# Input norm on one engine, a recurrence's products on VectorE, and two later tails in a hybrid decoder layer

## The chip, the cores and the metric

One core of a Trainium2 chip runs the kernel. The metric is the device time of one execution in microseconds (us). Engines are named as in the profile: PE (TensorE matmul), PEld (its weight load), DVE (VectorE), ACT (ScalarE), POOL (GpSimd), SP (SyncE, here only DMA issue). L12 is line 12 of the kernel.

## The reference

One decoder layer over 512 tokens of width 2048, in float32.

```
xn   = rmsnorm(x, norm_w);  proj = xn @ w_in          # 2048 -> all branches
# branch 1: HGRN2, 8 heads of 128: gated linear recurrence, then a norm per head
S_t  = diag(f_t) S_{t-1} + (1 - f_t) i_t^T ;  o_t = S_t^T q_t
o_hg = rmsnorm(o, hg_norm_w) * silu(z)
# branch 2: NSA, 4 key groups x 4 heads of 128, three attentions added by gates:
#   compressed blocks (31 keys), selected blocks, causal window
o_ns = g0 * softmax(q kc) vc + g1 * softmax(q ks) vs + g2 * softmax(q kw) vw
# merge
y    = x + (sig(m1) * (o_hg @ w_hg) + sig(m2) * (o_ns @ w_nsa)) @ w_out ; out = rmsnorm(y)
```

## The kernel before

Every float32 operand of a projection is split into a rounded high part and the rest, and a product is three matmuls: high x high, low x high, high x low (`mm3`). A weight block of 128 x 1024 is loaded by SP into one of three `wr` buffers, rounded by ACT (L130) and its rest taken by DVE (L131) into one of two `whl` buffers. A split of activations is the same pair, ACT L135 and DVE L136. So PE depends on a steady alternation of ACT and DVE whatever else these two do.

The stages follow one another: the start (L290 to L404, 0 to 61 us), projections that need no side work (to about 440 us), the recurrence (to about 855 us), compression of keys and values and the first branch product (to about 1077 us), the four key groups of NSA (to about 1660 us), the merge and the output product.

In the start, `normalise(i)` takes the square sum of token tile `i` (half on ACT L329, half on DVE L330), adds (DVE L335), takes the root (ACT L336), the reciprocal (DVE L337), and scales the tile by that and by the norm weight `nw`: quarters 0 and 1 in one DVE operation each (L341), quarters 2 and 3 first by `nw` on POOL (L334) and then by the scalar on DVE (L343). `transposed` turns each quarter on PE (L349) and splits it; `first` multiplies it with the first weight blocks.

From the recurrence on, `weave` runs two generators side by side: the projection of the next head or group (the main one), and the steps of the present one (`hg_core`, `nsa_core`), one step per `yield`, spread evenly over the main one's units. A scheduler then orders each engine's instructions, so the order on an engine differs from that in the code.

`hg_core` works on tiles of 128 channels x 512 tokens. `pre` and `suf` are products of decays up to and after a token within a block; `grow(h)` doubles the block, `suf` on POOL (L566) and `pre` on DVE (L567). `decayed(h)` forms the scaled keys (POOL L576) and queries (DVE L577) of a level in one tile `qk`, whose scores are transposed products on PE (L601) into a bank of PSUM, copied under a mask by DVE (L588, L590, L605) into `ad`. Seven levels follow one another. `kd` (POOL L624) and `qd` (DVE L625) serve the state. Last comes the norm of the head's output: ones-product on PE, root on ACT (L670), reciprocal and two products on DVE (L671 to L673), and a DMA issued by POOL (L674). It stands in the step behind the last products of the head, and falls beside the start of the next head.

`nsa_core(g)` does for each of four heads four steps of scores (query block i = 3, 2, 1, 0; L139 into `sc` banks, of which there are two), each followed by a masked maximum on DVE (L921), exponentials on ACT (L925) and a scale on POOL (L930); then six steps that transpose weights on PE (L949), split them (`pth`, `ptl`) and, one step later, multiply them with the values into the bank `po`. At a group's start the compressed part comes first: scores on PE, softmax on DVE and ACT (L864 to L888, tile `pc`), and the compressed values, loaded by ACT's queue (L855) into a tile `raw`, split into `vczh` and `vczl`. `nsa_proj(g)` loads the group's values into `vraw` (L822) and splits them whole.

PSUM has eight banks: three `pj`, two `sc`, two `pt`, one `po`.

## Time and profile before

| what | value |
|---|---|
| median of 3 runs | 2109.39 us (2108.59 to 2112.3) |
| profiled execution | 2108.82 us, span 2106.7 us, mean granted clock 0.996 |
| busy share | PE 98%, PEld 82%, DVE 57%, ACT 39%, POOL 15% |
| PE idle in 20-us windows, 0 to 40 us | 12.0 us |
| PE idle in 520 to 820 us | 7.4 us |
| PE idle in 1140 to 1580 us | 11.8 us |

The span is one profiled execution; the 2.1 us between it and the execution's own time lie outside the trace. PE's busy time is close to the span, so the time is read from where PE is idle. In the views, a bracket behind an instruction gives the idle time of its engine before it and the instruction whose end ended that. A window's row gives the busy time of each engine in it. All rows are of the one profiled execution.

### The profile page before, as it was taken

Reading aid. Unit: us, or ns where it says so; the run is one execution under the profiler, and the core shown is the slowest. Engines: PE = TensorE matmul, PEld = TensorE weight load, DVE = VectorE, ACT = ScalarE, POOL = GpSimd, SP = SyncE. Lnnn points to the kernel's source line nnn. Section 1 sums busy time; section 2 is a strip of 40 time slices with the busy share of each in tenths; the row PEclk is TensorE's granted clock in tenths of the full one; section 3 lists DMA queues with packets and bytes.
Section 4 is the critical chain, followed back from the end, with each engine's and each line's share of the span. In section 5 each row is a group of like instructions: output and inputs, shape, how many; then the busy total and the mean of one; then the engine's idle time right before and its main releaser. Section 6 shows DMA issues by size and latency. Waiting matters only on the chain.

```text
span 2106.7 us, 26671 instructions
## 1 busy us (share of the span) xinstructions
PE 2062.0 (98%) x10304; PEld 1721.2 (82%) x10304; DVE 1209.0 (57%) x1875; ACT 816.5 (39%) x1267; POOL 322.4 (15%) x411
## 2 busy tenths in 40 slices
PE   7999999999999999999999999999999999999998
PEld 6888888888888778878888887877878888888887
DVE  7687778745456655566545665657654453433333
ACT  4454444532233233344323444445445432222232
POOL 2000000003233432100002222213212100000000
PEclk9999999999999999999999999999999999999999
DMA  6325243332323222566752222222223394445232
GB/s 184 100 105 180 100 152 114 121 101 74 96 83 93 76 76 85 167 188 202 247 164 85 74 73 85 68 84 64 78 75 92 90 304 132 149 140 212 98 130 90
DMA packets 306595, 254.46 MB, mean 121 GB/s; under 512 B 10666, under 2 KB 263411, under 8 KB 305827
## 3 DMA queue, kind: packets, MB, share of 16 engines
q1 hardware_dynamic: 282980, 202.55, 31.8%
q0 software_dynamic: 8096, 26.28, 3.4%
q10 hardware_dynamic: 15392, 23.92, 3.3%
q8 instruction: 81, 1.33, 0.3%
q14 instruction: 46, 0.38, 0.1%
HBM read 222.25 MB, written 30.47 MB: 120 GB/s over the span
## 4 chain that ended last, share of the span: by engine, by line
PE 82%; DVE 7%; issue 4%; ACT 3%; DMA 3%; POOL 1%; SPq 0%; ACTq 0%; DVEq 0%; POOLq 0%
PE pj L139 17%; PE pj L141 17%; PE pj L140 17%; PE sc L214 4%; PE pt L214 4%; PE sc L215 2%; PE pt L215 2%; PE sc L141 2%; PE sc L139 2%; PE sc L140 2%; PE po L140 1%; DVE whl L131 1%; PE po L139 1%; PE po L141 1%; PE pt L949 1%
## 5 line engine op out<-in xcount | busy, mean ns | idle before, releaser
L139 PE MATMUL pj<-xhl,whl 128*128 128x512 f32 x1344 | 538.5, 401 | 0.0
L141 PE MATMUL pj<-xhl,whl 128*128 128x512 f32 x1344 | 527.7, 393 | 0.8 <-DVE whl L131 0.8
L140 PE MATMUL pj<-xhl,whl 128*128 128x512 f32 x1344 | 525.2, 391 | 0.0
L131 DVE TENSOR_TENSOR whl<-wr,whl 128x1024 fp32r<-128x1024 f32 x244 | 303.8, 1245 | 373.2 <-ACT whl L130 372.5
L130 ACT CAST whl<-wr 128x1024 fp32r<-128x1024 f32 x244 | 256.5, 1052 | 563.3 <-PE pj L141 446.8
L141 PEld LDWEIGHTS pj<-xhl,whl 128*128 128x128 f32 x1344 | 252.3, 188 | 56.6 <-DVE whl L131 2.0
L140 PEld LDWEIGHTS pj<-xhl,whl 128*128 128x128 f32 x1344 | 252.9, 188 | 46.4
L139 PEld LDWEIGHTS pj<-xhl,whl 128*128 128x128 f32 x1344 | 252.7, 188 | 46.1
L135 ACT CAST whl<-xt 128x1024 fp32r<-128x1024 f32 x75 | 78.6, 1052 | 97.7 <-PE pt L215 33.1
L136 DVE TENSOR_TENSOR whl<-xt,whl 128x1024 fp32r<-128x1024 f32 x75 | 91.5, 1223 | 39.3 <-ACT whl L135 39.2
L930 POOL TENSOR_SCALAR s<-s,sm 128x512 f32<-128x512 f32 (+3 forms) x128 | 82.2, 655 | 149.4 <-DVE sm L928 89.9
L139 PE MATMUL pj<-onh,whl 128*128 128x512 f32 x256 | 99.6, 389 | 0.0
L140 PE MATMUL pj<-onl,whl 128*128 128x512 f32 x256 | 99.6, 389 | 0.0
L141 PE MATMUL pj<-onh,whl 128*128 128x512 f32 x256 | 99.6, 389 | 0.0
L136 DVE TENSOR_TENSOR ptl<-pt,pth 128x512 fp32r<-128x512 f32 (+1 forms) x80 | 50.5, 633 | 69.3 <-ACT pth L135 68.6
L925 ACT ACTIVATE s<-s,mx 128x512 f32<-128x512 f32 (+3 forms) x128 | 70.9, 555 | 43.8 <-DVE mx L923 39.0
L135 ACT CAST pth<-pt 128x512 fp32r<-128x512 f32 (+1 forms) x80 | 43.5, 544 | 96.1 <-PE pt L949 95.7
L201 DVE TENSOR_TENSOR xt<-xt 128x1024 f32<-128x1024 f32 x64 | 77.5, 1219 | 0.6
L921 DVE CUSTOM_DVE_ANT_0 s<-sc,cf 128x512 f32<-128x512 f32 (+3 forms) x128 | 59.3, 483 | 20.1 <-PE sc L141 19.4
L698 POOL TENSOR_TENSOR rsh<-rsh,rope 32x512 f32<-32x512 f32 x28 | 42.2, 1507 | 183.8 <-DVE rsh L697 166.3
L566 POOL TENSOR_TENSOR suf<-suf,pre 128x256 f32<-128x256 f32 x56 | 51.8, 926 | 116.7 <-DVE pre L549 94.6
L131 DVE TENSOR_TENSOR cl<-wr,ch 128x1024 fp32r<-128x1024 f32 x32 | 39.1, 1223 | 44.6 <-ACT ch L130 44.6
(431 smaller groups left out, 4004.9 us busy)
## 6 DMA issues: line engine op xcount, KB each, us to landing
wr<-in_w_in_dram SPq DMA_DIRECT2D x172, 512.0 KB
xt<-in_w_in_dram SPq DMA_DIRECT2D x32, 1024.0 KB
wr<-in_w_branch_nsa_dram SPq DMA_DIRECT2D x32, 512.0 KB
wr<-in_w_out_dram SPq DMA_DIRECT2D x32, 512.0 KB
wr<-in_cmp_k_w_dram SPq DMA_DIRECT2D x16, 512.0 KB
wr<-in_w_branch_hg_dram SPq DMA_DIRECT2D x16, 512.0 KB
wr<-in_cmp_v_w_dram SPq DMA_DIRECT2D x16, 512.0 KB
gat_d<-wr POOLq DMA_DIRECT2D x20, 256.0 KB, 3.0
```

The source lines that it names most:

```text
L130: nc.scalar.copy(hi[:, :n], raw[:, :n])
L131: nc.vector.tensor_tensor(lo[:, :n], raw[:, :n], hi[:, :n].bitcast(F32), op=OP.subtract)
L135: nc.scalar.copy(hi, src)
L136: nc.vector.tensor_tensor(lo, src, hi.bitcast(F32), op=OP.subtract)
L139: nc.tensor.matmul(acc, lhsT=lh, rhs=rh, start=start, stop=False, **kw)
L140: nc.tensor.matmul(acc, lhsT=lh, rhs=rl, start=False, stop=False, **kw)
L141: nc.tensor.matmul(acc, lhsT=ll, rhs=rh, start=False, stop=stop, **kw)
L201: nc.vector.tensor_tensor(dst, dst, more, op=OP.add)
L214: nc.tensor.matmul(av, lhsT=l0, rhs=r, start=start, stop=False, skip_group_check=True)
L215: nc.tensor.matmul(av[:, 0], lhsT=l1, rhs=r[:, 0], start=False, stop=stop, skip_group_check=True)
L925: nc.scalar.activation(s[:, b], s[:, b], AF.Exp, scale=SCALE, bias=mx[:, b:b + 1], accum_out=sm[:, b:b + 1])
L930: nc.gpsimd.tensor_scalar(s[:, b], s[:, b], sm[:, b:b + 1], 1.0, op0=OP.mult, op1=OP.mult)
```

## The change

Four edits. (1) `normalise` scales all four quarters in one DVE operation each; the POOL product goes. (2) In the recurrence `suf`, the scaled keys and `kd` are formed by DVE. (3) The norm of a head is put into a list and done in the next head's steps behind its copy `kn`; the last head's at once. (4) In NSA the value products of a step are put into a list `due` and done later, those of the last steps in the next head's score steps; the compressed part's transposes stand one step earlier; one of the two score products of block 2 uses a `pj` bank; a group's values are loaded and split in two halves through the `raw` tiles; side steps are 46 and not 48.

```diff
@@ normalise
-            for k0 in (8, 12):
-                c = slice(k0 * P, (k0 + 4) * P)
-                nc.gpsimd.tensor_tensor(x[:, c], x[:, c], nw[:, c], op=OP.mult)
...
-                if k0 < 8:
-                    nc.vector.scalar_tensor_tensor(x[:, c], x[:, c], ss[:, :1], nw[:, c], op0=OP.mult, op1=OP.mult)
-                else:
-                    nc.vector.tensor_scalar(x[:, c], x[:, c], ss[:, :1], None, op0=OP.mult)
+                nc.vector.scalar_tensor_tensor(x[:, c], x[:, c], ss[:, :1], nw[:, c], op0=OP.mult, op1=OP.mult)
@@ hg_core
-                nc.gpsimd.tensor_tensor(fv[:, :, 0], fv[:, :, 0], whole(pv[:, :, 1]), op=OP.mult)
+                nc.vector.tensor_tensor(fv[:, :, 0], fv[:, :, 0], whole(pv[:, :, 1]), op=OP.mult)
...
-                nc.gpsimd.tensor_tensor(half(qk)[:, :, 0], half(kt)[:, :, 0], half(suf)[:, :, 0], op=OP.mult)
+                nc.vector.tensor_tensor(half(qk)[:, :, 0], half(kt)[:, :, 0], half(suf)[:, :, 0], op=OP.mult)
...
-            nc.gpsimd.tensor_tensor(kd, kt[:, :3 * P], suf[:, :3 * P], op=OP.mult)
+            nc.vector.tensor_tensor(kd, kt[:, :3 * P], suf[:, :3 * P], op=OP.mult)
...
             nc.scalar.copy(kn, ps[:, :3 * P])
             yield
+            if left:
+                left.pop()()
             yield
...
-            pm = lbank()
...
-            nc.gpsimd.dma_start(ohg_d[head], ow)
+            def normed():
+                pm = lbank()
...
+                nc.gpsimd.dma_start(ohg_d[head], ow)
+
+            left.append(normed)
+            if head == HG - 1:
+                left.pop()()
@@ nsa_proj
-        raw = ap.tile([P, 4, 2, DH], F32, name="vraw")
-        for b in range(2):
-            nc.scalar.dma_start(raw[:, :, b], v_d[1 + b, :, :, g * DH:(g + 1) * DH].rearrange("i p c -> p i c"))
...
-        split(f(vh), f(vl), f(raw))
+        for b in range(2):
+            raw = ap.tile([P, S], F32, name="raw", bufs=2)
+            rv = raw.rearrange("p (i c) -> p i c", i=4)
+            nc.scalar.dma_start(rv, v_d[1 + b, :, :, g * DH:(g + 1) * DH].rearrange("i p c -> p i c"))
+            split(vh[:, :, b], vl[:, :, b], rv)
@@ nsa_core
+        due = []
+        def pv_next():
+            if not due:
+                return
+            h, po, parts, hi, lo, last = due.pop(0)
+            for n, (j, b) in enumerate(parts):
+                w = slice(n * (4 - j) * P, (n + 1) * (4 - j) * P)
+                mm3(po[:, j * P:], vh[:, j, b], vl[:, j, b], hi[:, w], lo[:, w], False, last)
+            if last:
...
+                if i > 1:
+                    pv_next()
...
-                        ps = sbank()
+                        ps = bank() if i == 2 and b == 0 else sbank()
...
+                if h == 0 and i == 1:
+                    cmp_t()
...
-                    if pend:
-                        pv_mm(*pend, False)
-                    pend = (parts, hi, lo)
+                    if m == 2:
+                        po = psum("po")
+                        mm3(po, vcz[0][:, h], vcz[1][:, h], ph, pl, True, False)
+                    elif m > 2:
+                        pv_next()
+                    due.append([h, None, parts, hi, lo, m == 5])
...
+        while due:
             yield
+            pv_next()
+        yield
```

The program's order on DVE in the start, before and after the change (`xhl` are splits of a transposed quarter, `wfl` rests of the first weight blocks, the first `sq` is token tile 1's):

```order
-L330 SCALAR_TENSOR_TENSOR sq_269,ss<-xt 128x1024
-L343 TENSOR_SCALAR xt<-xt,ss 128x512 x2
-L335 TENSOR_TENSOR ss<-ss 128x1
-L337 RECIPROCAL ss<-ss 128x1
-L341 SCALAR_TENSOR_TENSOR xt<-xt,ss,nw 128x512 x2
-L131 TENSOR_TENSOR wfl<-wraw,wfh 128x1216
-L136 TENSOR_TENSOR xhl<-pt,xhl 128x4x128
```

```order
+L337 SCALAR_TENSOR_TENSOR xt<-xt,ss,nw 128x512 x4
 L131 TENSOR_TENSOR wfl<-wraw,wfh 128x1216
 L136 TENSOR_TENSOR xhl<-pt,xhl 128x4x128
 L131 TENSOR_TENSOR wfl<-wraw,wfh 128x1216
 L136 TENSOR_TENSOR xhl<-sc,xhl 128x4x128
```

Tile 0's last two quarters stood behind tile 1's square sum and now stand with the first two, ahead of the first weight block's rest.

DVE at the start of a head of the recurrence, before (`kt`, `pre` and `qf` begin the new head, `ob` and `ow` belong to the norm of the old one):

```order
L547 TENSOR_SCALAR kt<-sg,nomlb,omlb 128x512
L549 TENSOR_SCALAR pre<-sg,omlb,lbt 128x512
L552 TENSOR_TENSOR qf<-qf,pre 128x4x64
L671 RECIPROCAL ob<-ob 128x512
L567 TENSOR_TENSOR pre<-pre 128x256
L131 TENSOR_TENSOR whl<-wr,whl 128x1024
L672 SCALAR_TENSOR_TENSOR ow<-ow,sv,ob 128x512
L577 TENSOR_TENSOR qk<-qf,pre 128x128x2
L673 TENSOR_TENSOR ow<-ow,zs 128x512
```

The same place in the changed program, and then the place that the norm has come to, behind `kd` and `qd`, where the state `st` is formed:

```order
L542 TENSOR_SCALAR kt<-sg,nomlb,omlb 128x512
L544 TENSOR_SCALAR pre<-sg,omlb,lbt 128x512
L547 TENSOR_TENSOR qf<-qf,pre 128x4x64
L561 TENSOR_TENSOR suf<-suf,pre 128x256
L562 TENSOR_TENSOR pre<-pre 128x256
L571 TENSOR_TENSOR qk<-kt,suf 128x128x2
L572 TENSOR_TENSOR qk<-qf,pre 128x128x2
```

```order
L620 TENSOR_TENSOR qd<-qf,pre 128x384
L131 TENSOR_TENSOR whl<-wr,whl 128x1024 x2
L670 RECIPROCAL ob<-ob 128x512
L131 TENSOR_TENSOR whl<-wr,whl 128x1024
L671 SCALAR_TENSOR_TENSOR ow<-ow,sv,ob 128x512
L645 SCALAR_TENSOR_TENSOR st<-st,pre,sc 128x128
L672 TENSOR_TENSOR ow<-ow,zs 128x512
```

The old head's reciprocal and two products no longer stand among the new head's first operations; `suf` and the keys of `qk` stand there in their place.

ACT at the border from key group 0 to 1, before (`vh` are the group's values, `vczh` the compressed ones, `pc` the compressed scores, `s` the exponentials):

```order
L135 CAST vh<-vraw 128x1024
L130 CAST whl<-wr 128x1024
L178 ACTIVATE raw<-pj 128x512
L822 DMA vraw<-v_d 128x4x128
L855 DMA raw<-vc_d 31x128 x4
L864 COPY pc<-sc 128x512
L822 DMA vraw<-v_d 128x4x128
L135 CAST vczh<-raw 128x512
L879 ACT_TABLE_LOAD
L879 ACTIVATE pc<-pc 128x512
```

The same place in the changed program:

```order
L178 ACTIVATE raw<-pj 128x512
L828 DMA raw<-v_d 128x4x128
L135 CAST vh<-raw 128x4x128
L867 COPY pc<-sc 128x512
L828 DMA raw<-v_d 128x4x128
L858 DMA raw<-vc_d 31x128 x4
L135 CAST vh<-raw 128x4x128
L882 ACT_TABLE_LOAD
L882 ACTIVATE pc<-pc 128x512
L130 CAST whl<-wr 128x1024
L135 CAST vczh<-raw 128x512
L946 ACTIVATE s_9847,sm<-s_9847,mx 128x512 x2
```

A cast of `vh` now stands behind the DMA that brings its half, ahead of the copy of the compressed scores, and `vczh` has moved from ahead of the softmax of `pc` to between it and the first exponentials.

## Rows read from the trace of the kernel before

**Rows 1.** The page, part 1: busy time and share of the span.
```profile
PE 2062.0 (98%) x10304; PEld 1721.2 (82%) x10304; DVE 1209.0 (57%) x1875; ACT 816.5 (39%) x1267; POOL 322.4 (15%) x411
```

**Rows 2.** View of waits of PE: total us, times, longest us.
```profile
PE sc L139 <- DVE mx L921: 8.9, 6, 2.5
PE sc L601 <- DVE ad L605: 7.4, 7, 1.3
PE pt L349 <- DVE xt L341: 3.6, 1, 3.6
PE pt L349 <- DVE xt L343: 1.7, 1, 1.7
PE po L140 <- DVE ptl L136: 1.6, 3, 0.5
```

**Rows 3.** View of windows, the start: length, busy us (instructions) by engine, PEclk, DMA.
```profile
12.00:18.50 6.50, 6.49 (x25) 5.96 (x26) 5.73 (x7) 3.23 (x5) 0.00 (x0) 0.50 0.50 140
18.50:28.80 10.30, 5.98 (x30) 4.74 (x29) 8.47 (x9) 4.82 (x8) 5.31 (x4) 0.83 0.80 271
28.80:45.00 16.20, 13.22 (x94) 12.28 (x93) 15.88 (x22) 10.38 (x17) 6.78 (x5) 1.00 0.42 109
45.00:62.00 17.00, 16.83 (x117) 15.92 (x116) 16.60 (x23) 5.08 (x14) 0.00 (x0) 1.00 0.20 53
```

**Rows 4.** Timeline of POOL in the start: start, length, instruction, [idle before <-releaser].
```profile
18.62 5.31 POOL L334 TENSOR_TENSOR xt<-xt,nw 128x512 f32<-128x512 f32 x4 [7.45 <-issue]
```

**Rows 5.** Timeline of DVE in the start, same columns.
```profile
11.21 1.41 DVE L341 SCALAR_TENSOR_TENSOR xt<-xt,ss,nw 128x512 f32<-128x512 f32 x2 [2.67 <-POOL nw L305]
...
19.93 2.88 DVE L343 TENSOR_SCALAR xt<-xt,ss 128x512 f32<-128x512 f32 x2 [1.88 <-POOL xt L334]
...
22.73 1.22 DVE L335 TENSOR_TENSOR ss<-ss 128x1 f32<-128x1 f32 x1
...
25.84 1.42 DVE L131 TENSOR_TENSOR wfl<-wraw,wfh 128x1216 fp32r<-128x1216 f32 x1
...
32.47 0.68 DVE L136 TENSOR_TENSOR xhl<-pt,xhl 128x512 fp32r<-128x512 f32 x1
...
41.38 0.47 DVE L343 TENSOR_SCALAR xt<-xt,ss 128x512 f32<-128x512 f32 x1
```

**Rows 6.** Timeline of POOL behind the recurrence.
```profile
865.35 1.67 POOL L698 TENSOR_TENSOR rsh<-rsh,rope 32x512 f32<-32x512 f32 x1 [7.94 <-DMA rope<-in_cf_dram]
```

**Rows 7.** View of windows, a head of the recurrence.
```profile
720.00:740.00 20.00, 18.88 (x102) 16.02 (x101) 18.20 (x28) 3.64 (x4) 13.06 (x15) 1.00 0.25 75
```

**Rows 8.** Timeline of DVE, the same head.
```profile
718.87 3.34 DVE L671 RECIPROCAL ob<-ob 128x512 f32<-128x512 f32 x1
...
722.13 0.36 DVE L567 TENSOR_TENSOR pre<-pre 128x256 f32<-128x256 f32 x1
...
730.53 0.72 DVE L605 COPY_PREDICATED ad<-cm,sc 128x256 f32<-128x256 uint8 x1
...
746.55 1.22 DVE L131 TENSOR_TENSOR whl<-wr,whl 128x1024 fp32r<-128x1024 f32 x1 [6.28 <-ACT whl L130]
```

**Rows 9.** View of line L577 (queries of a level): ns min/median/max.
```profile
L577 DVE TENSOR_TENSOR qk<-qf,pre x48: 412/731/955, 479.7 to 823.7; 128x256 f32<-128x256 f32 x48
```

**Rows 10.** View of lines, POOL, 440 to 860 us: count | busy us, mean ns.
```profile
L566 POOL TENSOR_TENSOR suf<-suf,pre 128x256 f32<-128x256 f32 x56 | 51.8, 926 | 116.7 <-DVE pre L549 94.6 <-DVE pre L567 20.1 <-DVE ad L590 0.2
L576 POOL TENSOR_TENSOR qk<-kt,suf 128x256 f32<-128x256 f32 x48 | 44.2, 921 | 17.9 <-PE sc L601 6.3 <-PE pt L601 6.1 <-DVE ad L588 2.9
L624 POOL TENSOR_TENSOR kd<-kt,suf 128x384 f32<-128x384 f32 x8 | 10.6, 1320 | 0.6
```

**Rows 11.** Chain of waits at a border of key groups: start, length, what.
```profile
1275.89 6.63 DMA raw<-vc_d
```

**Rows 12.** View of windows after that border.
```profile
1280.00:1300.00 20.00, 16.67 (x77) 13.04 (x76) 14.72 (x45) 10.41 (x24) 6.80 (x9) 1.00 0.21 61
1300.00:1320.00 20.00, 20.00 (x103) 16.81 (x102) 11.34 (x19) 7.15 (x11) 2.49 (x3) 1.00 0.22 63
```

More of the change, by code (lines that the diff above doesn't have):

```diff
@@ L505, in body @@
         heads = {}
+        left = []
         def values(pr):
@@ L898, in nsa_core @@
         o3 = ap.tile([P, HPG, P], F32, name="o3")
+        due = []
[7 more added lines that the diff above has]
+            if last:
+                ow = ap.tile([P, 384], F32, name="ow", bufs=2)
+                nc.vector.tensor_copy(ow, po[:, :384])
+                nc.scalar.copy(o3[:, h], po[:, 384:])
+                nc.gpsimd.dma_start(ons_d[g * HPG + h][:, :384], ow)
         for h in range(HPG):
@@ L930, in nsa_core @@
                     nc.gpsimd.tensor_scalar(s[:, b], s[:, b], sm[:, b:b + 1], 1.0, op0=OP.mult, op1=OP.mult)
+                if h == 0 and i == 1:
+                    cmp_t()
                 yield
[L932 to L944 removed]
+            for m, parts in enumerate((((3, 0), (3, 1)), ((2, 0), (2, 1)), ((1, 0),), ((0, 0),), ((1, 1),), ((0, 1),))):
                 ps = tbank()
@@ L954, in nsa_core @@
                 else:
-                    hi = ap.tile([P, o], F32R, name=f"pth{o}", bufs=o // 256)
-                    lo = ap.tile([P, o], F32R, name=f"ptl{o}", bufs=o // 256)
+                    hi = ap.tile([P, o], F32R, name=f"pth{o}", bufs=2)
+                    lo = ap.tile([P, o], F32R, name=f"ptl{o}", bufs=2)
                     split(hi, lo, ps[:, :o])
-                    if pend:
-                        pv_mm(*pend, False)
-                    pend = (parts, hi, lo)
-                yield
-            pv_mm(*pend, True)
-            ow = ap.tile([P, 384], F32, name="ow", bufs=2)
-            nc.vector.tensor_copy(ow, po[:, :384])
-            nc.scalar.copy(o3[:, h], po[:, 384:])
-            nc.gpsimd.dma_start(ons_d[g * HPG + h][:, :384], ow)
+                    if m == 2:
[4 more added lines that the diff above has]
+                    due.append([h, None, parts, hi, lo, m == 5])
+                    if m >= 2:
+                        for d in due:
+                            d[1] = po
+                yield
+        while due:
             yield
+            pv_next()
+        yield
         ps = sbank()
@@ L979, in body @@
     for g in range(GROUPS - 1):
-        weave(nsa_proj(g + 1), 128, nsa_core(g), 48)
+        weave(nsa_proj(g + 1), 128, nsa_core(g), 46)
     def last():
@@ L984, in last @@
         yield from merge_gates(NG, NG + 6, ap, "raw")
-    weave(last(), 112, nsa_core(GROUPS - 1), 48)
+    weave(last(), 112, nsa_core(GROUPS - 1), 46)
     nsa.close()
```

24 lines of the change are left out of this document (6 added, 18 removed).

## The prediction

> **What bounds the kernel now.** I read the page first: PE is busy for 2062.0 of 2106.7 us [rows 1], so an edit on another engine can give back only what PE waits, 44.7 us in all. Where it waits stands in the view of waits [rows 2], and with the windows it falls into three places. In the start PE is busy for 42.5 of the 50 us from 12 to 62 [rows 3], which leaves 7.5 us; before 12 us it waits for the broadcast of the norm weight, which ends the wait of 3.6 us on L341 [rows 2] and which nothing here moves. In the recurrence it waits for DVE's masked copies, seven times, 7.4 us in all [rows 2]. In NSA it waits for the masked maxima, six times, 8.9 us, and three times, 1.6 us, for a split of weights [rows 2]. These are the places of the four edits. PE's own work does not change in amount: the matmuls are the same, so each term below is a change of idle time.
>
> **Start.** POOL's product (L334) begins at 18.62 after 7.45 us of idle time that no event ended [rows 4]. DVE stands 1.88 us before L343 for it, then takes 2.88 us for two scalings and 1.22 us for an addition of one column, with POOL running beside it; later, with POOL quiet, one L343 takes 0.47 [rows 5]. The Trainium skill, "SBUF — State Buffer", Who interferes with whom, gives a reason: VectorE and GpSimd share one port pair, and whoever holds it blocks the other. The rows agree (1.44 against 0.47 us for the same scaling); by that rule the four fused operations run at their own speed once POOL is silent.
> The replay of DVE's new order from 11.21: four fused scalings at 0.70 (L341, two in 1.41 [rows 5]) end at 14.0; two rests of weights at 1.34, three splits at 0.60 and one square sum of 1.15 follow, as they stood (start-to-start times of the same operations before), then a second square sum and the reciprocal, 1.3, and one scaling. The third weight block's rest begins at about 22.2, where it began at 25.84 [rows 5]: 3.6 us earlier. Tile 1's first split, at 32.47 before [rows 5], comes behind the fourth rest and three scalings, at about 27: 5.5 earlier. Behind that DVE is full before (15.88 of 16.2 and 16.60 of 17 us [rows 3]), and in this stretch and the one ahead of it its work shrinks: two pairs of scalings (the one at 19.93 takes 2.88, tile 1's is alike) come down to 1.41, about 2.9 us; three additions of one column like the one of 1.22 [rows 5], which cannot cost more than a few tenths undisturbed, give about 3; the wait of 1.88 goes; four scalings of 0.47 become 0.70, which costs 0.9. The sum is 6.9 us on DVE. PE can use at most its 7.5 of idle time. I take 5.5, since the first gaps (PE waiting for the transposes' splits) shrink by the 3.6 to 5.5 of the replay and not by all of DVE's sum. The bounds are 1.7 (only the wait on L343 [rows 2]) and 7.5. Of the clock: it is granted at 0.50 from 12 to 18.5, at 0.83 on average until 28.8, and fully behind [rows 3]; should the gap be followed by another stretch at the lower level, the gain falls toward its lower bound. POOL's 7.45 us [rows 4] look like something done once before its first product, and so move to POOL's next one, the rotation of keys behind the recurrence, whose engine idles for 7.94 us before it already, waiting for a table's DMA [rows 6]. I cost that at nothing; without that cover it would be at most 7.45 on POOL, of which PE, with a product beside it, would see about 2.
>
> **Recurrence.** In each of the seven heads that follow another, DVE takes the old head's reciprocal, 3.34 us, and two products of 1.34 and 0.68, together 5.4, between the new head's `qf` and its second level; the first of them and the `pre` behind it stand in [rows 8]. The window shows DVE busy for 18.20 of 20 us there [rows 7], and PE then waits for the masked copy at 730.53 [rows 8], 7.4 us over seven heads [rows 2]. The edit moves the 5.4 us to behind `qd`, beside 739 to 753, where DVE waits 6.28 us for a weight block [rows 8]. In their place DVE gets seven `suf`, six `qk` and one `kd` that took POOL 0.93, 0.92 and 1.32 us each [rows 10]. On DVE I price them by their twins: `pre` on the same shape at 0.36 (722.13, [rows 8]), the keys of `qk` by the queries, whose fastest take 0.41 [rows 9], at 0.43, `kd` at 0.55 (0.36 for 384 in place of 256 columns). That is 2.5 + 2.6 + 0.6 = 5.7 us, against 5.4 moved away; the bounds are 5.2 (all at 0.36, `kd` at 0.55) and 13.3 (POOL's own means). Besides, three waits for POOL of some 0.5 us each go, and the DVE operations that ran beside POOL (queries at a median of 0.73 [rows 9]) come nearer to 0.43, some 2 us. Replayed, the copy that released PE ends about 1.7 us earlier than it did, which is more than the longest wait of 1.3 [rows 2]: all 7.4 go. What comes late next is the state: the old head's 3.34 us reciprocal now stands ahead of the state's products on DVE, and PE's next state product waits for these. I give that 0.25 a head, 1.9 in all. Net: -5.5; bounds -7.4 and, with POOL's means for DVE's prices and no wait removed, +2.
> The Trainium skill, "Perfetto Trace Analysis", Optimizing Scalar/DVE Operations, speaks against this edit: with VectorE saturated, moving work off it, even to GpSimd, may make sense, and here work goes the other way onto an engine that is 91% busy [rows 7]. The same section warns that the two share a port, so that moving work between them might not help. By the first half the term would be about 0 or a loss (the rival below); by the rows the addition of 5.7 stands against 5.4 taken away, so I do not follow it.
>
> **NSA.** The value products of all heads are moved behind other work. In the middle of a group PE has no idle time (1300 to 1320 [rows 12]), so there is nothing to gain there; the three waits on `ptl`, 1.6 us [rows 2], go. What matters are the borders of groups: there PE is busy for 16.67 of 20 us [rows 12]. The chain runs through the compressed values' DMA, 6.63 us [rows 11], their split, then the softmax on DVE and the maxima. The change keeps this DMA and puts more around it: it now sits in ACT's queue behind the second half of the values, the cast of the first half stands on ACT behind its own DMA ahead of the copy of the compressed scores, and `vczh` stands ahead of the first exponentials. On the other hand DVE no longer stands at `vczl` before the reductions. With these durations I get stalls of about 2.9, 3.6, 3.8 and 4.1 us at the four group starts, against 0.8, 3.3 [rows 12], 2.5 and 3.5 before (the others read in the same windows): +4.3, less 1.6, is +2.7. The bounds: -8.9 if DVE's freedom removes the waits for maxima altogether [rows 2]; +10 if at three borders ACT stands for the whole DMA (3 x 6.63 [rows 11], less half of it that PE's queued projections cover).
>
> **Sum.** -5.5 - 5.5 + 2.7 = -8.3 on the profiled execution's 2108.82 us (2.1 us of it outside the span), so 2100.5. The median of the runs is 0.6 above the profiled execution; I leave the forecast at 2100.5 for both. A measurement of this kernel tells a difference of 0.2%, 4.2 us, from none, so faster means below 2105.2 and slower above 2113.6.
>
> **Rivals.**
> - DVE becomes the bound in the recurrence. For it: 91% busy in the critical window [rows 7]; against it: twins at 0.36 to 0.43. If the moved products cost POOL's means, DVE gets 13.3 - 5.4 = 7.9 us more per head in a window that has 1.8 free; the removed waits on POOL and the quieter neighbours return about 3.5. Some 2.6 us a head then fall on PE on top of today's waits, 7 x 2.6 = 18: with -5.5 of the start and +2.7 of NSA, 2124, slower. It decides from about 9.5 us of moved work a head on. Chance 4%.
> - The NSA borders. Price: the values' halves and the compressed values pass through two `raw` tiles; if each of three borders costs 4 us more than I have, the sum is +3.7 at most: 2112.5, no change. If the DMA's 6.63 us stands on ACT ahead of the exponentials at all four, with nothing queued on PE, +4 x 6.63 = 26.5, less 11 from the other two edits: 2124, slower. It decides from about 4 us a border on. For it: the wait behind the last maxima is already up to 2.5 [rows 2]; against it: PE has a projection of 128 units beside each group and needs ACT only every few us. Chance 5% slower, 8% no change.
> - The start gives little, as loads or the clock hold it: -1.7 in place of -5.5, and the recurrence gives only -3: with NSA 2106.8, no change. For it: a window at half clock [rows 3]; against it: DVE, not the loads, ended most waits [rows 2]. Chance 12%.
> - DVE's freedom removes the waits for maxima in NSA too: -5.5 - 5.5 - 7 gives 2091. For it: `vczl` no longer blocks the reductions; against it: the values' halves do. Chance 12%.
>
> **How the numbers follow.** The forecast holds 59%, with its own range 2096 to 2105 (the terms' half-way bounds). Faster: 59 + 12, plus 1 from the third rival's edge, 72%. Same: 19%. Slower: 9%. The range that leaves 2 in 10 outside runs from 2091 to 2109: it takes in the larger gain and the small start, and leaves out both slower cases and part of the no-change ones.
>
> **What would show it.** Right: the third weight rest near 22 us and no wait on L343; the stage's end (the last `first` product) 5 to 6 us earlier; no PE wait on the masked copies after the first head, and waits of 0.2 to 0.3 on the state instead; `suf` on DVE at 0.36 to 0.43; idle time of 2.5 to 4.5 at each group start. Wrong: PE waiting for masked copies as before or more (DVE saturated), waits above 6 us at a group start, or a start whose PE idle time stays above 5 us from 12 to 62.

## The result, and the profile after

The changed kernel takes 2085.72 us (median of 4 runs, 2083.59 to 2086.54) against 2108.99 (4 runs, 2107.38 to 2112.3): ratio 0.9886, 95% interval 0.9869 to 0.9903. That is 23.3 us less, where 8.3 were forecast and the range ended at 2091. The profiled execution's span is 2084.0 us, 22.7 less than before.

To see where they went, both traces were cut at the same products of PE: the starts of the same main projection products, counted along each trace. "Idle" is PE's idle time inside the stage.

| stage | before, us (idle) | after, us (idle) | difference | forecast |
|---|---|---|---|---|
| start and the first projections | 469.2 (14.3) | 463.2 (10.0) | -6.0 | -5.5 |
| recurrence | 400.6 (7.5) | 391.1 (0.0) | -9.5 | -5.5 |
| compression, first branch product | 244.1 (2.5) | 245.5 (2.4) | +1.4 | 0 |
| NSA to the output's first product | 634.8 (12.3) | 626.2 (7.2) | -8.6 | +2.7 |
| the rest | 358.0 (8.2) | 358.0 (8.2) | 0.0 | 0 |

The start is near its forecast, the recurrence has the right sign and gained 4.0 us more, NSA has the wrong sign. The page of the changed kernel, part 1, beside [rows 1]:

```profile
PE 2056.3 (99%) x10304; PEld 1724.4 (83%) x10304; DVE 1212.0 (58%) x1991; ACT 812.1 (39%) x1271; POOL 209.2 (10%) x291
```

PE's busy time fell by 5.7 us with the same 10304 matmuls, so a quarter of the gain does not appear as idle time. The rest, 17.0 us, is idle time. The waits of PE of the changed kernel, beside [rows 2] (total us, times, longest us):

```profile
PE pt L895 <- DVE mx L944: 3.0, 3, 1.3
PE pt L343 <- DVE xt L337: 2.4, 1, 2.4
PE pj L139 <- ACT wfh L130: 2.4, 1, 2.4
PE sc L139 <- DVE mx L942: 2.0, 1, 2.0
PE sc L139 <- ACT fh L135: 1.9, 1, 1.9
...
PE pt L871 <- ACT pc L867: 0.8, 1, 0.8
```

The waits on the masked copies of the recurrence and on `ptl` are gone; the maxima (L921, now L942) hold PE for 2.0 us and not 8.9, and in the transposes' line L895 3.0 us of waiting have come up.

**Start.** The windows, beside [rows 3], and VectorE's timeline, beside [rows 5], of the changed kernel:

```profile
12.00:18.50 6.50, 5.58 (x35) 4.38 (x36) 6.50 (x9) 4.30 (x7) 0.00 (x0) 1.00 0.60 200
18.50:28.80 10.30, 7.07 (x37) 6.35 (x36) 10.16 (x17) 4.13 (x6) 0.00 (x0) 0.83 0.85 253
28.80:45.00 16.20, 15.91 (x117) 15.12 (x116) 13.79 (x23) 10.44 (x20) 0.56 (x1) 1.00 0.59 158
```

```profile
11.12 2.74 DVE L337 SCALAR_TENSOR_TENSOR xt<-xt,ss,nw 128x512 f32<-128x512 f32 x4
...
20.17 0.16 DVE L332 TENSOR_TENSOR ss<-ss 128x1 f32<-128x1 f32 x1
...
22.25 1.42 DVE L131 TENSOR_TENSOR wfl<-wraw,wfh 128x1216 fp32r<-128x1216 f32 x1
...
26.91 0.68 DVE L136 TENSOR_TENSOR xhl<-pt,xhl 128x512 fp32r<-128x512 f32 x1
```

The four scalings take 0.69 each, the addition 0.16 where it took 1.22; the third weight rest starts at 22.25 (22.2 in the replay, 25.84 before) and tile 1's first split at 26.91 (about 27 in the replay, 32.47 before). From 12 to 18.5 us the granted clock is the upper level, 1.00 and not 0.50. From 12 to 45 us PE is idle 4.4 us, where it was 7.3. Another 1.2 us of the start's 4.3 us of idle time lie ahead of 12 us (4.7 before, 3.5 after), where the edit has changed nothing; the kernels below show 3.5 to 5.1 us there with either start.

**Recurrence.** The windows of the changed kernel, beside [rows 7], and the lines of VectorE over the stage (count | busy us, mean ns), beside [rows 9] and [rows 10]:

```profile
700.00:720.00 20.00, 20.00 (x104) 17.09 (x103) 14.93 (x33) 6.32 (x9) 1.08 (x2) 1.00 0.33 93
720.00:740.00 20.00, 20.00 (x117) 16.12 (x116) 11.02 (x17) 6.54 (x10) 0.53 (x1) 1.00 0.29 79
```

```profile
L562 DVE TENSOR_TENSOR pre<-pre 128x256 f32<-128x256 f32 x56 | 23.9, 427 | 1.3
L561 DVE TENSOR_TENSOR suf<-suf,pre 128x256 f32<-128x256 f32 x56 | 23.5, 419 | 0.0
L571 DVE TENSOR_TENSOR qk<-kt,suf 128x256 f32<-128x256 f32 x48 | 20.4, 425 | 0.0
L572 DVE TENSOR_TENSOR qk<-qf,pre 128x256 f32<-128x256 f32 x48 | 20.2, 420 | 0.0
...
L619 DVE TENSOR_TENSOR kd<-kt,suf 128x384 f32<-128x384 f32 x8 | 4.4, 552 | 0.0
```

PE is busy all through (the 20-us windows show 20.00). The products that took GpSimd 0.92 to 0.93 us take VectorE 0.42 (forecast 0.36 and 0.43), `kd` 0.55 as forecast. Queries came down from 0.65 to 0.42 on average.

**A border of key groups.** ACT and VectorE of the changed kernel at the border that [rows 11] and [rows 12] show before:

```profile
1260.34 0.62 ACT L135 CAST vh<-raw 128x512 fp32r<-128x512 f32 x1 [1.42 <-DMA raw<-v_d]
1261.48 0.59 ACT L867 COPY pc<-sc 128x512 f32<-128x512 f32 x1 [0.52 <-PE sc L141]
...
1265.07 1.34 ACTq L858 DMA_DIRECT2D raw<-vc_d  x4
1266.45 0.62 ACT L135 CAST vh<-raw 128x512 fp32r<-128x512 f32 x1 [4.38 <-DVE pc L881]
...
1269.90 0.62 ACT L135 CAST vczh<-raw 128x512 fp32r<-128x512 f32 x1
```

```profile
1266.06 0.69 DVE L942 CUSTOM_DVE_ANT_0 s<-sc,cf 128x512 f32<-128x512 f32 x1 [0.55 <-PE sc L141]
...
1271.51 0.68 DVE L136 TENSOR_TENSOR vczl<-raw,vczh 128x512 fp32r<-128x512 f32 x1
```

The DMA of the compressed values is now issued at 1265.07, ten microseconds into the border, but when ACT comes to their cast at 1269.90 it does not wait: it was busy with the softmax meanwhile. The first maximum (1266.06) stands ahead of the rest of that split (1271.51) on VectorE.

**Value products.** PE's timeline of one head, before and then after: the first two of the three matmuls on the weights of one block, 256 columns:

```profile
1225.37 0.37 PE L139 MATMUL po<-pth,vh 128*128 128x256 f32 x1
1225.75 0.38 PE L140 MATMUL po<-ptl,vh 128*128 128x256 f32 x1
```

```profile
1210.52 0.37 PE L139 MATMUL po<-pth,vh 128*128 128x256 f32 x1
1210.72 0.28 PE L140 MATMUL po<-ptl,vh 128*128 128x256 f32 x1
```

No idle time of PE is printed at either place. But the second begins 0.38 us behind the first before and 0.20 after. The weight load of the second shows why, and so do the waits of all these weight loads in NSA, both before the change:

```profile
1225.75 0.19 PEld L140 LDWEIGHTS po<-ptl,vh 128*128 128x128 f32 x1 [0.21 <-DVE ptl L136]
```

```profile
PEld po L140 <- DVE ptl L136: 4.6, 11, 0.7
```

The weight load stood 0.21 us for `ptl`, and the record of the first matmul covers that wait. In NSA the weight loads stand 4.6 us for `ptl`, of which PE's own rows show 1.6 [rows 2]; after the change they have no such wait. Taken from start to next start (cut at each record's end), the value products and those of the compressed values fill 70.3 us before and 67.2 after, for the same 336 matmuls.

**Compression.** The 1.4 us lost there are a stretch of the clock. Windows of the changed kernel:

```profile
880.00:884.50 4.50, 2.65 (x12) 1.75 (x10) 3.31 (x7) 1.76 (x3) 1.20 (x1) 1.00 0.71 214
884.50:888.00 3.50, 3.43 (x10) 2.46 (x9) 2.64 (x5) 2.32 (x4) 0.00 (x0) 0.51 0.37 139
```

PE waited 1.9 us for a split just ahead (1.7 before, at the same product), and for 3.4 us behind it the clock was granted at the lower level. The kernel before met the same wait without such a stretch; of the fifteen other kernels below, nine have one in this stage. With it the stage takes 245.5 to 246.6 us, without it 243.6 to 244.8: about 1.7 us, half the stretch.

### The profile page after: what moved, and what is told of

It reads as the page before. It is cut to its first block, busy times and chain, and to the rows that moved or that the text cites. A ratio compares the mean times of both kernels' runs of the same rounds, so it can differ in the third digit from the quotient of the medians.

```text
span 2084.0 us, 26532 instructions
## 1 busy us (share of the span) xinstructions
PE 2056.3 (99%) x10304; PEld 1724.4 (83%) x10304; DVE 1212.0 (58%) x1991; ACT 812.1 (39%) x1271; POOL 209.2 (10%) x291
## 3 DMA queue, kind: packets, MB, share of 16 engines
q8 instruction: 81, 1.33, 0.3%
## 4 chain that ended last, share of the span: by engine, by line
PE 87%; issue 5%; DVE 4%; DMA 2%; ACT 1%; POOL 1%; ACTq 0%; SPq 0%; DVEq 0%; POOLq 0%
PE pj L139 18%; PE pj L141 18%; PE pj L140 18%; PE sc L214 4%; PE pt L214 4%; PE sc L215 2%; PE pt L215 2%; PE sc L141 2%; PE sc L140 2%; PE sc L139 2%; PE po L139 1%; PE pt L960 1%; PE po L141 1%; PE po L140 1%; PE pj L214 1%
## 5 line engine op out<-in xcount | busy, mean ns | idle before, releaser
L131 DVE TENSOR_TENSOR whl<-wr,whl 128x1024 fp32r<-128x1024 f32 x244 | 299.0, 1226 | 393.5 <-ACT whl L130 393.5
L942 DVE CUSTOM_DVE_ANT_0 s<-sc,cf 128x512 f32<-128x512 f32 (+3 forms) x112 | 50.8, 474 | 29.1 <-PE sc L141 25.3
L701 POOL TENSOR_TENSOR rsh<-rsh,rope 32x512 f32<-32x512 f32 x28 | 48.2, 1720 | 142.0 <-DVE rsh L700 133.7
L130 ACT CAST ch<-wr 128x1024 fp32r<-128x1024 f32 x32 | 33.6, 1049 | 60.5 <-PE sc L141 39.0
```

The lines of the kernel that those rows point to most:

```text
L130: nc.scalar.copy(hi[:, :n], raw[:, :n])
L131: nc.vector.tensor_tensor(lo[:, :n], raw[:, :n], hi[:, :n].bitcast(F32), op=OP.subtract)
```

## The experiments

Ratios are to the kernel before, of runs on the same chip, with a 95% interval. Stages are cut as above, from one profiled execution each; a stretch of 3.4 us at half clock in one of them moves it by up to 1.7 us, so the start, which always holds one to five, is read by its idle time. How far profiles of one program scatter is read from the stages that a kernel leaves as they were: the old start has 10.4 to 14.3 us of idle time (seven kernels), the new one 9.5 to 10.0 (eight, GpSimd quiet); NSA takes 634.5 to 637.4 us (9.3 to 13.5 idle) unedited in six kernels and 626.1 to 626.9 (7.2 to 8.5) with all its edits in three.

| kernel | median us | ratio (interval) | start, idle | recurrence (idle) | NSA (idle) |
|---|---|---|---|---|---|
| before | 2108.99 | | 14.3 | 400.6 (7.5) | 634.8 (12.3) |
| start alone | 2104.31 | 0.9971 (0.9962-0.9981) | 10.0 | 400.4 (7.2) | 634.5 (9.3) |
| both edits of the recurrence | 2099.76 | 0.9952 (0.9937-0.9966) | 13.7 | 391.2 (0.0) | 637.4 (13.5) |
| late norm alone | 2103.04 | 0.9968 (0.9957-0.9979) | 13.3 | 393.0 (1.1) | 635.6 (10.7) |
| products alone | 2099.78 | 0.9953 (0.9938-0.9968) | 13.6 | 391.2 (0.0) | 635.4 (12.8) |
| NSA alone | 2099.78 | 0.9952 (0.9935-0.9968) | 10.6 | 400.6 (7.4) | 626.1 (8.5) |
| halves alone | 2104.56 | 0.9971 (0.9960-0.9982) | 13.7 | 400.7 (7.4) | 629.7 (7.8) |
| rest on GpSimd alone | 2101.96 | 0.9962 (0.9948-0.9976) | 10.4 | 400.7 (7.4) | 627.5 (6.3) |
| early GpSimd product | 2113.32 | 1.0013 (1.0003-1.0022) | 15.6 | 400.4 (7.2) | 636.0 (9.7) |
| changed | 2085.72 | 0.9886 (0.9869-0.9903) | 10.0 | 391.1 (0.0) | 626.2 (7.2) |
| changed, whole load | 2091.73 | 0.9918 (0.9903-0.9933) | 9.9 | 391.1 (0.0) | 633.4 (14.1) |
| changed, whole load, rest on GpSimd | 2086.87 | 0.9889 (0.9874-0.9904) | 9.7 | 391.2 (0.0) | 627.1 (8.7) |
| changed, no pj bank | 2085.76 | 0.9886 (0.9871-0.9901) | 9.6 | 391.1 (0.0) | 625.4 (5.9) |
| changed, values in step | 2087.84 | 0.9896 (0.9881-0.9911) | 9.6 | 391.1 (0.0) | 628.9 (8.1) |
| changed, transposes late | 2083.89 | 0.9871 (0.9854-0.9888) | 9.5 | 391.2 (0.0) | 623.7 (6.2) |
| the last, and rest on GpSimd | 2083.66 | 0.9878 (0.9863-0.9893) | 9.7 | 391.2 (0.0) | 624.2 (6.2) |
| changed, GpSimd busy in the start | 2090.34 | 0.9908 (0.9892-0.9925) | 12.9 | 391.2 (0.0) | 626.9 (7.7) |

### The three places by themselves

Each kernel is the one before with one group of the change's hunks, as they stand in its diff.

> The kernel before with the first edit alone (input norm on VectorE). Theory: the three gains are independent, so this one is what the changed kernel shows by the end of the start: the projections behind it begin 6.0 us earlier, PE's idle time is 4.3 us less there and the rest comes from the clock (0.50 before, 1.00 after, between 12 and 18.5 us); time 2103 us (ratio 0.997). Rival: part of it is given back later, because weights and tiles arrive at the same time as before; then the first product ends 6 us earlier and the time is within 3 us of before.

```diff
-            for k0 in (8, 12):
-                c = slice(k0 * P, (k0 + 4) * P)
-                nc.gpsimd.tensor_tensor(x[:, c], x[:, c], nw[:, c], op=OP.mult)
... and the four scalings as changed; nothing else
```

> The kernel before with both edits of the recurrence. Theory: no PE wait on the masked copies is left in the recurrence, 7.4 us less idle time, ratio 0.9963 (2101 us). Rival: the changed kernel's recurrence gains only because it starts at another phase of its weight loads; then waits of 3 us or more stay here.

> The kernel before with the edits of NSA alone. Theory: 8.6 us less (ratio 0.9959), of which 5.4 are PE idle time at the borders of key groups and 3.2 are waits inside the value products that the trace counts as busy time (mean of the first value matmul over 256 columns 0.197 before and 0.162 after). Rival: NSA gains only because the recurrence ends earlier and its loads then meet the borders differently; then under 4 us here.

Measured: -5.4, -10.0 and -10.0 us by medians, 25.4 together, against 23.3 of the whole; with intervals of plus or minus 2 to 3.5 us on each, the gains add up. The three rivals are out: the start's gain stands in the end time (4.0 to 8.0 us by its interval, where the rival had under 3), the recurrence keeps no wait, and NSA is 8.7 us shorter (3.8 of it idle time) without the earlier stages' shift. The start's length in that profile, 466.0, is 2.8 above the changed kernel's; it held 10.2 us at the lower clock against 3.4.

### The recurrence: norm or products

> The kernel before with the late norm of a head alone; the products stay on GpSimd. Theory: the 5.4 us of the norm in front of the new head's decays are what made PE wait, so this alone removes 6 to 7.4 us of the 7.4 (ratio 0.9967). Rival: the chain from GpSimd's products to VectorE and back is what made it late; then at least half of the 7.4 us stays.

```diff
+            if left:
+                left.pop()()
... and normed() as changed; nothing else
```

> The kernel before with the recurrence's products on VectorE and the norm where it was. Theory: VectorE is then over-full at the start of a head (18.2 of 20 us, and 5.7 more), so PE's waits on the masked copies do not go, and grow from 7.4 to 10 us or more in the recurrence; ratio 1.000 to 1.003. Rival: GpSimd's products and the port it shares with VectorE were the delay; then the waits fall below 4 us even with the norm in place.

```diff
-                nc.gpsimd.tensor_tensor(fv[:, :, 0], fv[:, :, 0], whole(pv[:, :, 1]), op=OP.mult)
+                nc.vector.tensor_tensor(fv[:, :, 0], fv[:, :, 0], whole(pv[:, :, 1]), op=OP.mult)
... and so qk's keys and kd; nothing else
```

The first expectation held (7.5 us of idle time became 1.1). The second failed, and with it the balance that the prediction had drawn. With the norm still in front of the head, the products on VectorE alone leave no wait at all: the stage takes 391.2 us, as with both. The late norm alone also does nearly the whole (393.0), and on top of the products it adds nothing (391.2 with, 391.2 without). VectorE's waits over the stage, in the kernel before, with the late norm alone, and with the products alone:

```profile
DVE pre L567 <- POOL suf L566: 14.1, 26, 0.8
```

```profile
DVE pre L568 <- POOL suf L567: 27.0, 43, 0.8
```

```profile
DVE ad L605 <- PE pt L601: 7.4, 13, 0.9
```

Before, VectorE stands 14.1 us for GpSimd's `suf`, 1.8 a head, and its own operations beside GpSimd are longer (queries 0.65 on average, 0.42 without). With the late norm it comes to the levels sooner and stands 27.0 us for `suf`. With the products it waits for PE's scores in the levels instead: the chain is no longer late. The windows of the stage, before and with the products alone:

```profile
469.20:869.80 400.60, 393.13 (x2180) 328.56 (x2179) 229.64 (x321) 124.77 (x173) 120.89 (x136) 1.00 0.30 87
```

```profile
469.90:861.10 391.20, 391.20 (x2181) 329.06 (x2180) 240.29 (x433) 124.75 (x173) 13.94 (x24) 1.00 0.32 90
```

VectorE's busy time rises by only 10.7 us, 1.3 a head, because its other operations get shorter and the records of operations in a row overlap a little; and 1.8 a head of waits for `suf` go. So 6.0 us of products a head on VectorE cost it less than a chain that went to GpSimd and back at each of seven levels.

One reading of the kernel before was incomplete. PE's rows name VectorE's masked copy as what ended its seven waits, but the weight loads of the same products name GpSimd's keys at six of them:

```profile
PEld sc L601 <- POOL qk L576: 9.4, 6, 1.7
```

At each of the six the keys and the copy end within about 0.1 us of each other. By these ends an earlier copy alone would have gained about 0.1 us a wait; with either remedy the weight loads wait for no keys any more. Whether the hop between the engines, the longer product on GpSimd or the slowing side by side weighs most was not separated.

### NSA: which piece

> The changed kernel with the load of a group's values as before: one tile of its own, split whole; the two smaller kinds of transposed weights then have one buffer again (there is no room for two). In the program's order the split of the compressed values then stands ahead of the softmax on VectorE again. Theory: that split, waiting for its DMA of 5 to 7 us, is what made VectorE late at the borders, so 3 to 5 us of PE idle time return at the borders of groups (6.5 us of idle time in NSA become about 10) and the ratio to before goes from 0.989 to about 0.991. Rival: the borders gained by the extra bank; then idle time in NSA stays near 6.5 us.

```diff
+        raw = ap.tile([P, 4, 2, DH], F32, name="vraw")
+        for b in range(2):
+            nc.scalar.dma_start(raw[:, :, b], v_d[1 + b, :, :, g * DH:(g + 1) * DH].rearrange("i p c -> p i c"))
...
+        split(f(vh), f(vl), f(raw))
...
-                    hi = ap.tile([P, o], F32R, name=f"pth{o}", bufs=2)
+                    hi = ap.tile([P, o], F32R, name=f"pth{o}", bufs=o // 256)
```

NSA goes back to 633.4 us and 14.1 of idle time, 6.9 more where 3 to 5 were expected. VectorE of this kernel at the border, the rest of the compressed values' split:

```profile
1265.96 0.69 DVE L136 TENSOR_TENSOR vczl<-raw,vczh 128x512 fp32r<-128x512 f32 x1 [3.87 <-ACT vczh L135]
```

It stands 3.87 us for `vczh`, ahead of the first reduction. So the two halves of the load, which the prediction charged as a cost, carry most of the gain. Two kernels tell whether by the load or by this order:

> The kernel before with one piece of the NSA edits alone: a group's values loaded and split in two halves through the raw tiles. The program's order then has the split of the compressed values behind the softmax on VectorE and ACT. Theory: PE's idle time in NSA (12.3 us before) falls to 5 to 7, ratio 0.997. Rival: the halves need the second buffers of the transposed weights or the moved value products beside them; then 10 us or more of idle time stay.

```diff
-        raw = ap.tile([P, 4, 2, DH], F32, name="vraw")
+        for b in range(2):
+            raw = ap.tile([P, S], F32, name="raw", bufs=2)
... as nsa_proj is changed; nothing else
```

> The kernel before with the rest of the compressed values' split (vczl) taken by GpSimd in place of VectorE; loads and everything else as before. It takes VectorE's wait for that split away without touching a load. Theory: VectorE reaches the softmax and the maxima 3 to 4 us earlier at each border, PE's waits on the masked maxima (8.9 us) fall to under 4, idle time in NSA from 12.3 to about 8 (ACT still stands for the DMA ahead of the softmax's exponentials). Rival: the DMA of the values themselves, or ACT, is what makes the borders late; then idle time stays at 11 us or more.

```diff
-        split(vcz[0].rearrange("p h d -> p (h d)"), vcz[1].rearrange("p h d -> p (h d)"), raw)
+        f_ = lambda t: t.rearrange("p h d -> p (h d)")
+        nc.scalar.copy(f_(vcz[0]), raw)
+        nc.gpsimd.tensor_tensor(f_(vcz[1]), raw, f_(vcz[0]).bitcast(F32), op=OP.subtract)
```

VectorE at the border from group 0 to 1 in the kernel before (the split's rest, then the first maximum); with the halves alone (the first maximum, then the rest); with the rest on GpSimd (the first maximum); and GpSimd there:

```profile
1283.32 0.69 DVE L136 TENSOR_TENSOR vczl<-raw,vczh 128x512 fp32r<-128x512 f32 x1 [3.74 <-ACT vczh L135]
...
1285.26 0.68 DVE L921 CUSTOM_DVE_ANT_0 s<-sc,cf 128x512 f32<-128x512 f32 x1
```

```profile
1283.75 0.69 DVE L921 CUSTOM_DVE_ANT_0 s<-sc,cf 128x512 f32<-128x512 f32 x1 [0.55 <-PE sc L141]
...
1288.90 0.69 DVE L136 TENSOR_TENSOR vczl<-raw,vczh 128x512 fp32r<-128x512 f32 x1
```

```profile
1280.92 0.69 DVE L923 CUSTOM_DVE_ANT_0 s<-sc,cf 128x512 f32<-128x512 f32 x1 [0.55 <-PE sc L141]
```

```profile
1282.68 1.29 POOL L858 TENSOR_TENSOR vczl<-raw,vczh 128x512 fp32r<-128x512 f32 x1 [6.53 <-ACT vczh L857]
```

With the rest on GpSimd the first maximum starts at 1280.92, 4.3 us sooner than at 1285.26, with the loads as before; NSA gets 7.3 us shorter (627.5) and loses 6 of idle time. With the halves the rest moved behind the maximum and NSA gets 5.1 us shorter (629.7); this kernel's NSA began 2.0 us later, so its first maximum is 3.5 us sooner within the stage. Both theories held: the halves leave a little more idle time (7.8) than the 5 to 7 expected, GpSimd less (6.3) than the 8. With the rest on GpSimd ACT still stands for the same DMA, ahead of the softmax's exponentials:

```profile
1281.92 0.62 ACT L857 CAST vczh<-raw 128x512 fp32r<-128x512 f32 x1 [4.99 <-DMA raw<-vc_d]
```

So it was VectorE's standing for the split, and not ACT's for the DMA, that the border paid for.

> The changed kernel with the values loaded and split whole again (and one buffer for the two smaller transposed weights), and the rest of the compressed values' split on GpSimd. Theory: the halves are worth 5 to 7 us only because they put that split behind the softmax on VectorE; with it on GpSimd the whole load costs nothing, so NSA takes 626 to 628 us (633 with the whole load and the split on VectorE) and the ratio is 0.988 to 0.989. Rival: the halves also bring the values or the softmax earlier; then NSA stays at 630 us or more.

Measured 627.1 us, with one stretch of 3.4 us at half clock in it, as in the changed kernel's 626.2: the whole load, its single buffers included, costs nothing once VectorE does not stand for the split, though ACT stands 5.3 us for the DMA at this border. The halves' worth is the order.

> The changed kernel with all score products in the two sc banks, as before. Theory: VectorE is no longer blocked, so the third bank is worth little: 1 to 2 us more idle time at the borders. Rival: the bank is what removed the waits for maxima; then 4 us or more of waits on the masked maxima return.

```diff
-                        ps = bank() if i == 2 and b == 0 else sbank()
+                        ps = sbank()
```

No effect (ratio 0.9886 both; NSA 625.4). Both of its theories gave the bank more than it has.

> The changed kernel with the value products one step behind their weights, inside their head, as before; the rest of NSA as changed. Theory: the waits that the trace counts as busy time return, 3 to 5 us (the first value matmul over 256 columns goes from 0.16 back to 0.20 us on average, the sum over NSA by about 3), idle time at the borders stays as in the changed kernel. Rival: the borders gain from these products as filler between scores; then idle time in NSA rises by 3 us or more and the busy time does not.

```diff
+            po = psum("po")
+            mm3(po, vcz[0][:, h], vcz[1][:, h], ph, pl, True, False)
             for m, parts in enumerate((((3, 0), (3, 1)), ((2, 0), (2, 1)), ((1, 0),), ((0, 0),), ((1, 1),), ((0, 1),))):
...
+                    pv_next()
+                    due.append([h, po, parts, hi, lo, m == 5])
                 yield
+            pv_next()
```

NSA takes 628.9 us, 2 to 3 more than in the three kernels with all its edits. The value products fill 69.8 us again (67.2 with the delay, 70.3 before), which is 2.6, and idle time is 0.9 above the changed kernel's, inside the scatter. By medians the loss is 2.1 us, inside the intervals: the profile shows the mechanism, the time alone does not.

> The changed kernel with the transposes of the compressed part in a step of their own behind the first head's scores, as before. Theory: no effect beyond 1 us (the wait of the transposes, 3.0 us in three places in the changed kernel, turns into less waiting there, up to 2 us gained). Rival: the value products wait for the split that follows; then 2 us or more are lost.

```diff
-                if h == 0 and i == 1:
-                    cmp_t()
                 yield
+            if h == 0:
+                cmp_t()
+                yield
```

> The changed kernel with two differences: the compressed part's transposes in a step of their own behind the first head's scores, and the rest of the compressed values' split on GpSimd. A candidate to beat both kernels. Theory: VectorE is already free of that split in the changed kernel, so only the transposes' waits go: 1 to 3 us under the changed kernel (ratio to before about 0.987, idle time in NSA about 5.5). Rival: moving the split again gives another 3 us or more, because the border still waits for it.

NSA takes 623.7 and 624.2 us with 6.2 of idle time, against 626.1 to 626.9 in the three kernels with all its edits: about 2 to 3 us better by the profiles for the transposes' old place, and nothing more for the rest on GpSimd. By this the early place of the transposes, part of the change, costs rather than gains. The medians are 1.8 and 2.1 us below the changed kernel's, and the intervals overlap widely (0.9863 to 0.9893 and 0.9869 to 0.9903). No kernel here is shown to beat the changed one.

### The start: order or neighbour

> The kernel before with one tiny product on GpSimd at the very start (its result is not used). Theory: the 7.45 us in which GpSimd idled before its first product are spent once, so L334 starts by about 12 us and not at 18.6, VectorE's wait for it and PE's wait of 1.7 us on L343 go, and the start's idle time falls by 1.5 to 3 us of the 4.3 that the first edit gives; the rest needs VectorE undisturbed. Rival: it is the order on VectorE and not GpSimd's lateness; then L334 starts earlier and PE's idle time in the start stays within 1 us.

```diff
+        dum = sp.tile([P, 8], F32, name="dum")
+        nc.gpsimd.memset(dum, 1.0)
+        nc.gpsimd.tensor_tensor(dum, dum, dum, op=OP.mult)
```

GpSimd's timeline in that kernel:

```profile
1.15 0.19 POOL L307 TENSOR_TENSOR dum<-dum 128x8 f32<-128x8 f32 x1 [0.31 <-POOL dum L306]
9.81 2.30 POOL L308 PARTITION_BROADCAST nw<-xt  x1 [8.47 <-ACT sq L332]
19.65 10.61 POOL L337 TENSOR_TENSOR xt<-xt,nw 128x512 f32<-128x512 f32 x6 [7.54 <-issue]
```

The small product started at once, and the 7.5 us stand again between the broadcast and the first large product: they follow the broadcast and are not the cost of a first use. At the head of this time GpSimd's sequencer takes two instructions that are not in the kernel's text, here at 12.0 us and in the kernel before at 11.1 (ns min/median/max, first to last start):

```profile
L334 POOLq MODIFY_POOL_CONFIG  x2: 129/129/129, 11.1 to 11.1; - x2
```

That these cause the wait was not tested. The edit also moved VectorE's program order: two weight rests and tile 1's square sum now stand ahead of the first scalings, which begin later (at 11.21 before):

```profile
15.65 1.41 DVE L344 SCALAR_TENSOR_TENSOR xt<-xt,ss,nw 128x512 f32<-128x512 f32 x2
```

So neither theory's number can be read from this kernel, and its median of 3.6 us more than before says nothing of the product itself.

> The changed kernel with eight unused products of 128x512 on GpSimd beside the start (they read the norm weight only, no instruction waits for them; VectorE's order is the same). Theory: two-input products of GpSimd slow VectorE's operations, so VectorE's scalings and additions between 19 and 30 us lengthen (0.70 to 1 us or more, 0.16 to 1.2) and the start gives back 1.5 to 3 us of its 6. Rival: the order on VectorE alone gave the 6 us; then the start's length stays within 1 us of 463.

```diff
+            for c0 in (0, 512):
+                dm = sp.tile([P, 512], F32, name="dm", bufs=2)
+                nc.gpsimd.tensor_tensor(dm, nw[:, c0:c0 + 512], nw[:, c0:c0 + 512], op=OP.mult)
```

VectorE and GpSimd of that kernel in the start:

```profile
12.02 2.74 DVE L340 SCALAR_TENSOR_TENSOR xt<-xt,ss,nw 128x512 f32<-128x512 f32 x4 [3.52 <-POOL nw L305]
...
21.34 0.80 DVE L335 TENSOR_TENSOR ss<-ss 128x1 f32<-128x1 f32 x1
...
23.40 1.33 DVE L340 SCALAR_TENSOR_TENSOR xt<-xt,ss,nw 128x512 f32<-128x512 f32 x1
24.65 2.26 DVE L131 TENSOR_TENSOR wfl<-wraw,wfh 128x1216 fp32r<-128x1216 f32 x1
```

```profile
19.11 13.76 POOL L334 TENSOR_TENSOR dm<-nw 128x512 f32<-128x512 f32 x8 [7.13 <-issue]
```

Ahead of 19.11, with GpSimd quiet, four scalings take 2.74 us; beside it one takes 1.33, a weight rest 2.26 and not 1.42, the addition 0.80 and not 0.16. The start's idle time goes from 10.0 to 12.9 us and its length from 463.2 to 466.5. Part of this can be a later broadcast (the scalings begin at 12.02, not 11.12); but from 12 us to 62 PE idles 7.3 us here and 2.7 to 4.4 in the eight other kernels with this start, so a busy GpSimd alone, VectorE's order kept, brings 2 us or more of idle time back. How much of the first edit's gain is the order's was not run by itself. The rule of the Trainium skill, "SBUF — State Buffer", Who interferes with whom, that the two engines hold the shared ports against each other, agrees with these rows.

## Why the prediction was right and wrong

**Start: right.** Forecast -5.5, measured -6.0 in the profile and -5.4 alone, by the steps named: no wait on L343, the weight rest and tile 1's split within 0.1 us of the replay. That the profile's number is so close is partly luck: 1.2 us of it lie ahead of 12 us, where the prediction moved nothing, and the start held 10.2 us at the lower clock before and 3.4 after. One remark beside it was half wrong: the 7.45 us of GpSimd are no cost of its first product but follow the broadcast. That they cost nothing is as forecast: no GpSimd product of the start is left to wait for them, and in the changed kernel the two MODIFY_POOL_CONFIG stand at 843.2 us, ahead of the rotation of keys, whose 8.25 us of idle time (7.94 before) end with the table's DMA.

**Recurrence: the direction right, the reason only in part.** All 7.4 us of waits went, as forecast. The charge of 1.9 us for the state's products was wrong: PE has no idle time in the stage (and 0.25 us over seven heads would be 1.75). Besides, 2.0 us came off PE's busy time; the weight loads' waits for GpSimd's keys, 9.4 us where PE's rows show 7.4, fit that. The balance "5.7 stands against 5.4 taken away" was not what decided: with 6.0 us added and nothing taken away the waits vanish as well. What the prediction held for a side gain, the waits for GpSimd (1.8 us a head) and the slower operations beside it (6.0 us of products raise VectorE's busy time by 1.3 a head), pays for the products by itself. The prediction also read only VectorE's copy as what holds PE, where GpSimd's keys ended beside it. The rival "VectorE becomes the bound" is out, and with it, for this kernel, the first half of the rule that the prediction takes from the Trainium skill ("Perfetto Trace Analysis", Optimizing Scalar/DVE Operations) and that speaks for moving work to GpSimd. That the two engines share a port agrees with the longer operations side by side; the warning that a move between them might not help does not hold here.

**NSA: wrong, and this is the step that made the forecast fail.** The prediction put stalls of 2.9, 3.6, 3.8 and 4.1 us at the group starts, because the DMA of the compressed values sat deeper in ACT's queue and the casts ahead of the exponentials. Measured are 0.8, 1.3, 1.2 and 2.5 us, and NSA's idle time fell from 12.3 to 7.2. ACT does not wait for that DMA any more, since it comes to the cast only after the softmax's exponentials; and where it still does, with the rest on GpSimd, the border does not pay for it. "VectorE no longer stands at `vczl` before the reductions" stood in the text as a minor credit, with its full price, 8.9 us, only as the lower bound; it was the main effect: 5.1 us by the halves alone and 7.3 by GpSimd alone. The rival that held it (2091, 12%) had the mechanism.

The second half of the miss is the sentence that in the middle of a group there is nothing to gain since PE has no idle time there. The records of matmuls cover short waits: the value products gave 3.1 us of PE's busy time besides the 1.6 of idle time that the prediction counted, and the weight loads' waits of 4.6 us for `ptl` stood in the trace of the kernel before.

Together: -8.6 in place of +2.7 is 11.3 of the 14.4 us between forecast and span; the recurrence's 4.0 are the next term, the start 0.5; the clock in the compression stage took 1.4 back.

## What to carry to other kernels

An early wait is paid by everything that the program has put behind it on the same engine (here 3.7 us on VectorE ahead of the first maximum): before pricing a DMA that comes later, look whether the instruction that waits for it now stands behind useful work instead of ahead of it. A chain that hops between two engines at every level can be slower than all of it on the busier one, as it was here, where the two also slowed each other down. And a busy share of 100% does not show that PE is not waiting: read the waits of its weight loads too, and compare the distance between starts of a repeated group with its shortest one.

## What was not expected of the hardware

GpSimd idles 6.8 to 7.6 us between the partition broadcast and its next product, also where a product ran before the broadcast; two MODIFY_POOL_CONFIG instructions stand at the head of that time. The granted clock fell to the lower level (1.2 GHz) for 3.4 us behind a wait of PE of 1.9 us (the changed kernel, compression) and not behind waits of 1.7 and 2.1 us in the same place (the kernel before, halves alone); such a stretch moves a stage by about 1.7 us, and the start alone held between 3.4 and 17.1 us at that level.
